# A two-layer macaron trunk on one core: joint hi|lo products in the feed-forward blocks, an unscaled up half, and both tiles' down products in one row

## The chip, the cores and the metric

The kernel runs on one core of one Trainium2 chip. The metric is device microseconds of one execution, the median of several runs. The engines are named as the profile names them: PE is TensorE (PEld its weight loads), DVE is VectorE, ACT is ScalarE, POOL is GpSimd, SP is the queue from which all weights are fetched.

## What is computed

The reference is two layers, each a half-step gated feed-forward block, a token mixer (a causal convolution module in layer 0, a gated linear recurrence in layer 1) and a second feed-forward block, all with a norm ahead and a norm behind. The sequence has 256 tokens of width 1024, and the inner width of a feed-forward block is 2816. What the change touches:

```python
def rms_norm(x, gain):
    y = x32 * lax.rsqrt(jnp.mean(x32 * x32, axis=-1, keepdims=True) + EPS)
    return (y * gain)
def swiglu_ffn(x, w_in, w_out):
    gate, up = jnp.split(x @ w_in, 2, axis=-1)
    return (jax.nn.silu(gate) * up) @ w_out
...
for layer in range(DEPTH):
    h = swiglu_ffn(rms_norm(x, g[0]), ffn_w_in[layer, 0], ffn_w_out[layer, 0])
    x = x + 0.5 * rms_norm(h, g[1])
    ...                                   # token mixer
    h = swiglu_ffn(rms_norm(x, g[4]), ffn_w_in[layer, 1], ffn_w_out[layer, 1])
    x = x + 0.5 * rms_norm(h, g[5])
```

## The kernel before

**Numbers as pairs.** Every float32 operand of a large product is split into a rounded part and the rest (`split`, lines 131 to 133: one ACT cast to `wh` or `hi`, one DVE subtraction to `wl` or `lo`), and a product is three matmuls: hi·hi, hi·lo, lo·hi.

**Tiles.** The 256 tokens are two tiles of 128. `xth` and `xtl` (lines 100 and 101) hold the turned, gained but not yet normed input of a block, all 8 blocks k of 128 channels of tile 0 and then of tile 1; `xkh` and `xkl` are views that give block k of both tiles, so two pieces of 128 elements. The norm factor r of a token is applied to the products, not to the input.

**A feed-forward block** (`ffn`, from line 348) walks through 11 chunks of 256 inner channels. The weights of a chunk are six transfers of 128x1024 (`fetch`: four `w1`, two `w2`), each landing in a `raw` buffer (4 of them) and split into a `wh` and a `wl` buffer (10 each). Chunk 0 is multiplied with the tokens as rows (`project`, `up`, `turn`). Chunks 1 to 10 are multiplied with the channels as rows: `up_both(c, b)` with b = 0, 1 takes a block of 128 gate channels and the 128 up channels that belong to it. It calls `channels` (line 319), which makes, in the two halves of one PSUM bank `mm`, 24 matmuls each for gate and up: 8 blocks k times three matmuls of 256 columns. One DVE step (line 332) then multiplies both halves by the tokens' factors `scales` into `ga`. ACT takes the sigmoid (line 386), DVE multiplies twice (387, 388), and `split` makes the hidden pair in `both[c]`, a `b4` buffer. `down(t, c)` multiplies the hidden pair of tile t with `w2[c]`, 12 matmuls of 512 columns into two `acc` banks.

**Order.** The loop of line 419 writes `up_both(c, 0)`, `down(0, c-1)`, `up_both(c, 1)`, `down(1, c-1)`. A scheduler orders each engine's queue from this; PE, ACT, DVE and SP each run their own queue strictly in its order and wait for each other by semaphores. Within ACT's and DVE's queues the splits of coming weights stand between the steps that evacuate `channels`. PSUM has four `acc`, two `mm` and two `tr` banks; `tr` serves transposes, the spectrum of the convolution's taps in the first block, and small sums.

**Ends.** `post_norm` forms the closing norm of a block: ACT's sums of squares, a POOL addition of D·EPS and a power (`rsqrt`), then x is updated. `mean_square` makes the factor r of the next block on the same two engines, and `start` puts the two together. The recurrent mixer also calls `channels` (`forget`, `query`, 8 calls); the four feed-forward blocks call it 80 times.

Of the kernel before, what the change touches and what calls it, by code (L numbers as in the profile page):

```python
# [16 lines left out]
P = 128  # L17
# [23 lines left out]
def trunk_kernel(  # L41
# [33 lines left out]
    def narrow(tag, dtype=F32):  # L75
        return new(sb, [P, 256], dtype, tag, {"e": 4, "hid": 4}[tag])
# [75 lines left out]
    def mean_square(src):  # L152
# [7 lines left out]
        return rsqrt(tot, 1.0 / D, EPS)  # L160

    def pre_norm(t, gi):
        src = xs[t]
        hi, lo = xth[:, t * D : (t + 1) * D], xtl[:, t * D : (t + 1) * D]
        for h in range(2):
# [4 lines left out]
            for j in range(4):  # L170
                k = h * 4 + j
                g = gcol[:, gi * KD + k : gi * KD + k + 1]
                act.activation(hi[:, k * P : (k + 1) * P],
                               pt[:, j * P : (j + 1) * P], AF.Copy, scale=g)
            for j in range(4):
                k = h * 4 + j
                g = gcol[:, gi * KD + k : gi * KD + k + 1]
                sl = slice(k * P, (k + 1) * P)
                dve.scalar_tensor_tensor(
                    lo[:, sl], pt[:, j * P : (j + 1) * P], g, hi[:, sl].bitcast(F32),  # L180
# [4 lines left out]
    def boot():  # L185
# [14 lines left out]
        def turned(i):  # L200
            src = part(pieces, i)
            nc.sync.dma_start(src, x_turned[i])
            for j in range(2):
# [3 lines left out]
                act.activation(xkh[:, k], xk, AF.Copy, scale=g)  # L207
                dve.scalar_tensor_tensor(xkl[:, k], xk, g, xkh[:, k].bitcast(F32),
                                         op0=ALU.mult, op1=ALU.subtract)

        def multiply(t, i):
            wh, wl = ws[i]
            hi, lo = xth[:, t * D : (t + 1) * D], xtl[:, t * D : (t + 1) * D]
            for k in (2 * i, 2 * i + 1):
                sl = slice((k % 2) * 512, (k % 2) * 512 + 512)
                kp = slice(k * P, (k + 1) * P)
                mm3(o[t], hi[:, kp], lo[:, kp], wh[:, sl], wl[:, sl], k == 0, k == KD - 1)

        for i in range(4):
            with behind(act, dve, pe, nc.sync):  # L220
                turned(i)
# [7 lines left out]
            if i == 3:  # L229
                with behind(dve, pe):  # L230
# [5 lines left out]
                    pool.tensor_tensor(r, ms, mhalf[:, :NT], op=ALU.pow)  # L236
            with behind(pe):
                multiply(1, i)
        xt = [(xth[:, t * D : (t + 1) * D], xtl[:, t * D : (t + 1) * D], r[:, t : t + 1])
              for t in range(NT)]  # L240
# [14 lines left out]
    def post_norm(t, accs, gain, share, bias=None):  # L255
# [16 lines left out]
        r = rsqrt(ss[:, 0:1], ss[:, 1:2], D * EPS, op=ALU.add)  # L272
# [6 lines left out]
    def project(t, xt, ws):  # L279
        o = mm()  # L280
        hi, lo, _ = xt
        for h in range(2):
            todo = []
            for k in range(h * 4, h * 4 + 4):
                wh, wl = ws[k // 2]
                sl = slice((k % 2) * 512, (k % 2) * 512 + 512)
                kp = slice(k * P, (k + 1) * P)
                pe.matmul(o, hi[:, kp], wh[:, sl], start=k == 0, stop=False)  # L288
                pe.matmul(o, hi[:, kp], wl[:, sl], start=False, stop=False)  # L289
                todo.append((lo[:, kp], wh[:, sl]))  # L290
# [4 lines left out]
    def blocks(hi, lo, n):  # L295
        return [(hi[:, k * P : (k + 1) * P], lo[:, k * P : (k + 1) * P]) for k in range(n)]
# [22 lines left out]
    def channels(ws, cols_, scales):  # L319
        o = mm()  # L320
        for part in range(2):
            og = o[:, part * SEQ : (part + 1) * SEQ]
            for k in range(KD):
# [3 lines left out]
                pe.matmul(og, wh[:, cs], xkh[:, k], start=k == 0, stop=False)  # L327
                pe.matmul(og, wh[:, cs], xkl[:, k], start=False, stop=False)  # L328
                pe.matmul(og, wl[:, cs], xkh[:, k], start=False, stop=k == KD - 1)  # L329
# [6 lines left out]
    def start(gi, before):  # L336
# [4 lines left out]
        with behind(act):  # L341
            r = [mean_square(xs[0])]
        second = pre_norm(1, gi)
        with behind(act):
            r.append(mean_square(xs[1]))
        return [(*first, r[0]), (*second, r[1])]

    def ffn(layer, which, before, extra=None):
        base = layer * 3 + (0 if which == 0 else 2)
        accs = [None, None]  # L350
        w1, w2, hid, raw, both = {}, {}, {}, {}, {}
# [567 lines left out]
```

## Time and profile before

| | |
|---|---|
| time, median of 3 runs | 1020.4 us (1019.01 to 1020.74) |
| the profiled execution's own time | 1019.7 us |
| its span, first to last instruction | 1017.9 us |
| PE busy | 1003.4 us, 99% of the span |
| DVE, ACT busy | 711.0 us (70%), 503.3 us (49%) |
| mean granted TensorE clock | 0.995 |

Matmuls overlap in the records: one of 256 columns is 281 ns long on the average, but the next starts after less than half of that. How long a stage takes is therefore read from the starts of its first and of the next stage's first matmul, not from the sum of lengths. An engine's idle time counts only where PE then waits for it.

### The profile page before, as it was taken

The numbers are of one execution on the slowest core, as the hardware profiler recorded it, in microseconds if no ns is written. First come the engines' busy times: TensorE is split into PE (matmuls) and PEld (weight loads), VectorE is DVE, ScalarE is ACT, GpSimd is POOL, SyncE is SP. The second block draws the span as 40 slices with busy tenths as digits, with TensorE's granted clock in tenths as the row PEclk, the third lists the DMA queues.
The fourth block names the chain that finished last, engine by engine and source line by source line (L and its number), as shares of the span: only waits on it lengthen the run. The fifth ranks groups of instructions, "written<-read, shape, count | busy, mean of one in ns | idle before, by whom it ended". The sixth has DMA issues, their size and how long they took to land.

```text
span 1017.9 us, 16846 instructions
## 1 busy us (share of the span) xinstructions
PE 1003.4 (99%) x6692; PEld 916.1 (90%) x6692; DVE 711.0 (70%) x1114; ACT 503.3 (49%) x840; POOL 47.0 (5%) x85
## 2 busy tenths in 40 slices
PE   9999999999899999999999999999999999999997
PEld 7999999888779999999899999989998889999996
DVE  6766756899787575658675757687788595656563
ACT  7554534764485444446554535474143473535341
POOL 1000000010010000000200000020000110000000
PEclk9999999999899999999999999999999999999999
DMA  7885564742536565657455555665233565565541
GB/s 251 270 272 180 173 209 155 266 172 90 186 103 212 184 202 171 201 172 236 157 174 199 190 183 181 211 201 173 85 124 105 165 195 178 166 207 170 203 145 42
DMA packets 50958, 182.19 MB, mean 179 GB/s; under 512 B 6048, under 2 KB 6176, under 8 KB 50880
## 3 DMA queue, kind: packets, MB, share of 16 engines
q1 hardware_dynamic: 50736, 181.09, 53.8%
q8 instruction: 52, 0.85, 0.3%
q14 instruction: 26, 0.21, 0.1%
q10 hardware_dynamic: 144, 0.03, 0.0%
HBM read 180.06 MB, written 1.05 MB: 178 GB/s over the span
## 4 chain that ended last, share of the span: by engine, by line
PE 94%; DVE 2%; ACT 1%; DMA 1%; POOL 1%; issue 0%; DVEq 0%; POOLq 0%; SPq 0%; ACTq 0%
PE mm L327 16%; PE mm L328 16%; PE mm L329 16%; PE acc L137 9%; PE acc L136 9%; PE acc L138 9%; PE mm L288 4%; PE mm L289 4%; PE mm L292 4%; PE tr L630 2%; DMA raw<-wts 1%; PE tr L169 1%; DVE wl L133 1%; PE tr L136 1%; PE tr L138 1%; PE tr L137 1%
## 5 line engine op out<-in xcount | busy, mean ns | idle before, releaser
L133 DVE TENSOR_TENSOR wl<-raw,wh 128x1024 fp32r<-128x1024 f32 (+1 forms) x386 | 400.9, 1061 | 197.5 <-ACT wh L132 193.6
L132 ACT CAST wh<-raw 128x1024 fp32r<-128x1024 f32 (+1 forms) x386 | 337.5, 922 | 278.7 <-PE mm L328 128.8
L327 PE MATMUL mm<-xth,wh 128*128 128x256 f32 x1408 | 396.2, 281 | 0.3 <-ACT wh L132 0.3
L329 PE MATMUL mm<-xth,wl 128*128 128x256 f32 x1408 | 396.1, 281 | 0.0
L328 PE MATMUL mm<-xtl,wh 128*128 128x256 f32 x1408 | 396.0, 281 | 0.0
L327 PEld LDWEIGHTS mm<-xth,wh 128*128 128x128 f32 x1408 | 265.7, 189 | 3.8 <-DVE e L387 0.7
L328 PEld LDWEIGHTS mm<-xtl,wh 128*128 128x128 f32 x1408 | 265.1, 188 | 2.5
L329 PEld LDWEIGHTS mm<-xth,wl 128*128 128x128 f32 x1408 | 266.1, 189 | 0.1
L136 PE MATMUL acc<-wh,b 128*128 128x512 f32 x352 | 138.0, 392 | 0.0
L137 PE MATMUL acc<-wl,b 128*128 128x512 f32 x352 | 137.4, 390 | 0.0
L138 PE MATMUL acc<-wh,b 128*128 128x512 f32 x352 | 137.4, 390 | 0.0
L138 PEld LDWEIGHTS acc<-wh,b 128*128 128x128 f32 x352 | 66.1, 188 | 14.4
L136 PEld LDWEIGHTS acc<-wh,b 128*128 128x128 f32 x352 | 66.1, 188 | 11.4
L137 PEld LDWEIGHTS acc<-wl,b 128*128 128x128 f32 x352 | 66.1, 188 | 11.4
L386 ACT ACTIVATE e<-ga 128x256 f32<-128x256 f32 x80 | 33.4, 418 | 78.4 <-DVE ga L332 78.4
L288 PE MATMUL mm<-wh,xth 128*128 128x512 f32 x176 | 70.8, 402 | 0.0
L289 PE MATMUL mm<-wl,xth 128*128 128x512 f32 x176 | 70.0, 398 | 0.0
L332 DVE TENSOR_TENSOR ga<-mm,scales 128x512 f32<-128x512 f32 x88 | 60.4, 686 | 11.5 <-PE mm L329 11.4
L132 ACT CAST b<-e 128x256 fp32r<-128x256 f32 x80 | 32.4, 405 | 51.4 <-DVE e L388 51.4
L147 POOL TENSOR_SCALAR tiny<-tiny 128x1 f32<-128x1 f32 (+1 forms) x28 | 8.5, 302 | 918.8 <-ACT b L269 736.3
L292 PE MATMUL mm<-wh,xtl 128*128 128x512 f32 x176 | 49.3, 396 | 0.0
L133 DVE TENSOR_TENSOR b<-e,b 128x256 fp32r<-128x256 f32 x80 | 33.8, 423 | 20.8 <-ACT b L132 20.8
(164 smaller groups left out, 864.5 us busy)
## 6 DMA issues: line engine op xcount, KB each, us to landing
raw<-wts SPq DMA_DIRECT2D x328, 512.0 KB, 5.2
b<-rows SPq DMA_DIRECT2D x10, 512.0 KB, 6.8
b<-x_turned SPq DMA_DIRECT2D x4, 256.0 KB, 5.8
x<-x_in SPq DMA_DIRECT2D x2, 512.0 KB, 7.4
out_dram<-x SPq DMA_DIRECT2D x4, 256.0 KB, 2.0
b<-dft SPq DMA_DIRECT2D x1, 371.0 KB, 6.0
ca<-masks SPq DMA_DIRECT2D x1, 192.0 KB, 3.5
b<-w_dw SPq DMA_DIRECT2D x1, 128.0 KB, 6.2
```

The source lines that it names most:

```text
L132: act.copy(dst_h, src)
L133: dve.tensor_tensor(dst_l, src, dst_h.bitcast(F32), op=ALU.subtract)
L136: pe.matmul(o, lh, rh, start=first, stop=False)
L137: pe.matmul(o, lh, rl, start=False, stop=False)
L138: pe.matmul(o, ll, rh, start=False, stop=last)
L288: pe.matmul(o, hi[:, kp], wh[:, sl], start=k == 0, stop=False)
L289: pe.matmul(o, hi[:, kp], wl[:, sl], start=False, stop=False)
L292: pe.matmul(o, a, w, start=False, stop=h == 1 and n == 3)
L327: pe.matmul(og, wh[:, cs], xkh[:, k], start=k == 0, stop=False)
L328: pe.matmul(og, wh[:, cs], xkl[:, k], start=False, stop=False)
L329: pe.matmul(og, wl[:, cs], xkh[:, k], start=False, stop=k == KD - 1)
L332: dve.tensor_tensor(pair(res), pair(o), scales.unsqueeze(1).broadcast_to([P, 2, SEQ]), op=ALU.mult)
```

## The change

1. `xth` and `xtl` become one tile `xt` in the order block k, part (hi or lo), tile, so that hi and lo of block k for both tiles are 512 adjacent elements; `turned(t)` gives the views of one tile. Two unused tiles of 88 and 40 floats stand ahead of and behind it.
2. `channels` multiplies a hi weight block with the whole of these 512 columns (hi·hi in the left half of a bank, hi·lo in the right), 8 matmuls, and then the lo weight block with the 256 hi columns, 8 matmuls into the left half. Gate and up now have a bank each, `mm` and `tr`. ACT copies the right half to an `e` buffer, DVE adds it to the left, and only the gate is multiplied by `scales`. `e` has 6 buffers for 4. The mixer keeps the old form under the name `channel_pair`.
3. The up half thus stays without the factor r (in `up` too), so the hidden values and the sums of `down` are short of one factor r per token. The closing norm divides by the root of the mean square plus EPS, so it gives the same when EPS is divided by r squared: `mean_square` and `boot` store D·EPS times (mean square + EPS) in `floors`, one more POOL step per tile and block, and `post_norm` adds that in place of the constant.
4. The loop writes `up_both(c, 0)`, `up_both(c, 1)`, `down(0, c-1)`, `down(1, c-1)`.

```diff
-        return new(sb, [P, 256], dtype, tag, {"e": 4, "hid": 4}[tag])
+        return new(sb, [P, 256], dtype, tag, {"e": 6, "hid": 4}[tag])
...
-    xth = const.tile([P, NT * D], F32R, name="xth")
-    xtl = const.tile([P, NT * D], F32R, name="xtl")
-    xkh = xth.rearrange("p (t k m) -> p k t m", t=NT, m=P)
-    xkl = xtl.rearrange("p (t k m) -> p k t m", t=NT, m=P)
+    const.tile([P, 88], F32, name="before_xt")
+    xt_all = const.tile([P, NT * 2 * D], F32R, name="xt")
+    const.tile([P, 40], F32, name="after_xt")
+    xhl = xt_all.rearrange("p (k s t m) -> p k s t m", t=NT, s=2, m=P)
...
+    def turned(t):
+        return [xhl[:, :, s, t, :] for s in range(2)]
...
-    def rsqrt(ss, scalar, eps, n=1, op=ALU.mult):
+    def rsqrt(ss, scalar, eps, n=1, op=ALU.mult, floor=None):
         t = tiny(n)
         pool.tensor_scalar(t, ss, scalar, eps, op0=op, op1=ALU.add)
+        if floor is not None:
+            pool.tensor_scalar(floor, t, D * EPS, None, op0=ALU.mult)
...
-        r = rsqrt(ss[:, 0:1], ss[:, 1:2], D * EPS, op=ALU.add)
+        r = rsqrt(ss[:, 0:1], ss[:, 1:2], floor, op=ALU.add)
...
     def channels(ws, cols_, scales):
+        res = wide("ga")
+        for part, bank in enumerate((mm, tr)):
+            o = bank()
+            pair = o.rearrange("p (s t m) -> p s t m", s=2, m=P)
+            block = lambda w, k: w[:, (k % 2) * 512 + cols_[part] : (k % 2) * 512 + cols_[part] + P]
+            for k in range(KD):
+                pe.matmul(pair, block(ws[k // 2][0], k), xhl[:, k], start=k == 0, stop=False)
+            for k in range(KD):
+                pe.matmul(pair[:, 0], block(ws[k // 2][1], k), xhl[:, k, 0],
+                          start=False, stop=k == KD - 1)
+            cross = narrow("e")
+            act.copy(cross, o[:, SEQ:])
+            dve.tensor_tensor(res[:, part * SEQ : (part + 1) * SEQ], o[:, :SEQ], cross, op=ALU.add)
+        dve.tensor_tensor(res[:, :SEQ], res[:, :SEQ], scales, op=ALU.mult)
+        return res
+
+    def channel_pair(ws, cols_, scales):
         o = mm()
...
-            dve.scalar_tensor_tensor(h, o[:, CH:], r, g, op0=ALU.mult, op1=ALU.mult)
+            dve.tensor_tensor(h, o[:, CH:], g, op=ALU.mult)
...
             up_both(c, 0)
             if c == 1:
                 turn(1, 0)
+            up_both(c, 1)
             if c < NC - 1:
                 down(0, c - 1)
-            up_both(c, 1)
             if c < NC - 2:
                 down(1, c - 1)
...
-        post_norm(0, accs[0], gain, 0.5)
+        post_norm(0, accs[0], gain, 0.5, floor=floors[0])
```

How the instructions stand on the engines, in a chunk in the middle of a block. On PE before, the end of one block's product (the last of the 8 blocks k of its up half), the head of tile 0's down row, whose six rows for the second block of the hidden pair follow in the same way, and the next product's start:

```order
L327 MATMUL mm_3931<-xth,wh_3914 128x256
L328 MATMUL mm_3931<-xtl,wh_3914 128x256
L329 MATMUL mm_3931<-xth,wl_3915 128x256
L136 MATMUL acc_3459<-wh_3745,b_659_3755 128x512
L137 MATMUL acc_3459<-wl_3746,b_659_3755 128x512
L138 MATMUL acc_3459<-wh_3745,b_659_3755 128x512
...
L327 MATMUL mm_4000<-xth,wh_3896 128x256
L328 MATMUL mm_4000<-xtl,wh_3896 128x256
L329 MATMUL mm_4000<-xth,wl_3897 128x256
```

On PE after, the up half of the second block's product, the heads of the rows of tile 0 (`acc_3327`) and tile 1 (`acc_3341`), and the next chunk's first product:

```order
L331 MATMUL tr_3932<-xt,wh_3828 128x512 x2
L331 MATMUL tr_3932<-xt,wh_3834 128x512 x2
L331 MATMUL tr_3932<-xt,wh_3840 128x512 x2
L331 MATMUL tr_3932<-xt,wh_3846 128x512 x2
L333 MATMUL tr_3932<-xt,wl_3829 128x256 x2
...
L140 MATMUL acc_3327<-wh_3695,b_766_3705 128x512
...
L140 MATMUL acc_3341<-wh_3695,b_766_3705 128x512
...
L331 MATMUL mm_4021<-xt,wh_3985 128x512 x2
L331 MATMUL mm_4021<-xt,wh_3991 128x512 x2
```

A product's 24 matmuls of one half have become 8 wide and 8 narrow ones, all hi weights are used before the first lo weight, and 24 matmuls of `down` stand together between two chunks.

On ACT, one chunk's work before (casts of weights `wh`, sigmoids `e`, casts of the hidden pair `b`):

```order
L132 CAST b_784_4630<-e_4682 128x256
L132 CAST wh_4783<-raw_4781 128x1024
L132 CAST wh_4789<-raw_4787 128x1024
L132 CAST wh_4795<-raw_4793 128x1024
L132 CAST wh_4801<-raw_4799 128x1024
L386 ACTIVATE e_4751<-ga_4749 128x256
L132 CAST wh_4934<-raw_4932 128x1024
L132 CAST b_784_4630<-e_4751 128x256
```

And after, from the copy of the second product's gate half on:

```order
L336 COPY e_3929<-mm_3912 128x256
L136 CAST wh_3997<-raw_3995 128x1024
L136 CAST wh_4003<-raw_4001 128x1024
L136 CAST wh_4009<-raw_4007 128x1024
L336 COPY e_3949<-tr_3932 128x256
L410 ACTIVATE e_3953<-ga_3911 128x256
L136 CAST wh_4015<-raw_4013 128x1024
L136 CAST b_797_3862<-e_3953 128x256
L136 CAST wh_4142<-raw_4140 128x1024
```

The copy of the up half (`tr_3932`) now stands behind three casts of the next chunk's weights, and the sigmoid behind that copy.

## Rows read from the trace of the kernel before

**Rows 1.** Page, busy time: us, share of the span, instructions of each engine.
```profile
PE 1003.4 (99%) x6692; PEld 916.1 (90%) x6692; DVE 711.0 (70%) x1114; ACT 503.3 (49%) x840; POOL 47.0 (5%) x85
```

**Rows 2.** Page, chain that ended last, its shares of the span by engine.
```profile
PE 94%; DVE 2%; ACT 1%; DMA 1%; POOL 1%; issue 0%; DVEq 0%; POOLq 0%; SPq 0%; ACTq 0%
```

**Rows 3.** Windows, second block's chunks: from:to, length, busy per engine, clock, DMA share, GB/s.
```profile
310.00:480.00 170.00, 170.00 (x1201) 159.84 (x1201) 110.44 (x153) 80.05 (x114) 0.88 (x2) 1.00 0.60 197
```

**Rows 4.** Timeline, PE, where products and down rows begin: start, us, engine, line, what.
```profile
333.70 0.28 PE L327 MATMUL mm<-xth,wh 128*128 128x256 f32 x1
...
339.40 0.40 PE L136 MATMUL acc<-wh,b 128*128 128x512 f32 x1
...
342.14 0.28 PE L327 MATMUL mm<-xth,wh 128*128 128x256 f32 x1
...
347.84 0.40 PE L136 MATMUL acc<-wh,b 128*128 128x512 f32 x1
...
350.58 0.28 PE L327 MATMUL mm<-xth,wh 128*128 128x256 f32 x1
...
354.74 0.28 PE L329 MATMUL mm<-xth,wl 128*128 128x256 f32 x1
354.85 0.28 PE L327 MATMUL mm<-xth,wh 128*128 128x256 f32 x1
```

**Rows 5.** Chain in order of time: start, us, projection and convolution matmuls.
```profile
217.77 0.24 PE tr L136 x2
...
830.02 0.93 PE mm L292 x4
```

**Rows 6.** Groups by form: line, engine, what, count, busy us, mean ns, idle before; last: timeline.
```profile
L133 DVE TENSOR_TENSOR wl<-raw,wh 128x1024 fp32r<-128x1024 f32 x270 | 326.0, 1222 | 188.9 <-ACT wh L132 187.5
L132 ACT CAST wh<-raw 128x1024 fp32r<-128x1024 f32 x270 | 272.0, 1050 | 251.7 <-PE mm L328 126.8 <-DMA raw<-wts 106.4 <-PE mm L292 8.3
L332 DVE TENSOR_TENSOR ga<-mm,scales 128x512 f32<-128x512 f32 x88 | 60.4, 686 | 11.5 <-PE mm L329 11.4
L387 DVE TENSOR_TENSOR e<-e,ga 128x256 f32<-128x256 f32 x80 | 33.8, 423 | 18.7 <-ACT e L386 18.7
L502 DVE TENSOR_TENSOR b<-tr,b 128x256 f32<-128x256 f32 x8 | 3.4, 422 | 2.1 <-PE tr L138 2.0
...
310.56 0.36 ACT L316 COPY scales<-tr 128x256 f32<-128x256 f32 x1
```

**Rows 7.** Timeline, ACT and DVE, weight splits of one chunk; in brackets the idle before.
```profile
337.39 3.90 ACT L132 CAST wh<-raw 128x1024 fp32r<-128x1024 f32 x4 [3.12 <-PE mm L328]
...
338.47 2.36 DVE L133 TENSOR_TENSOR wl<-raw,wh 128x1024 fp32r<-128x1024 f32 x2 [3.74 <-ACT wh L132]
```

**Rows 8.** Page, DMA issues: count, KB each, us from issue to landing.
```profile
raw<-wts SPq DMA_DIRECT2D x328, 512.0 KB, 5.2
```

**Rows 9.** Timeline, start of the second block's chunk 1 on PE, ACT and DVE.
```profile
307.64 0.37 PE L327 MATMUL mm<-xth,wh 128*128 128x256 f32 x1
...
312.79 1.06 ACT L132 CAST wh<-raw 128x1024 fp32r<-128x1024 f32 x1 [0.20 <-DMA raw<-wts]
...
312.62 2.48 DVE L133 TENSOR_TENSOR wl<-raw,wh 128x1024 fp32r<-128x1024 f32 x2 [0.72 <-ACT wh L132]
```

**Rows 10.** Timeline, first block's chunks 1 and 2 on PE, ACT and DVE.
```profile
19.11 0.28 PE L327 MATMUL mm<-xth,wh 128*128 128x256 f32 x1
...
19.56 1.13 ACT L132 CAST wh<-raw 128x512 fp32r<-128x512 f32 x2
...
20.96 2.17 ACT L132 CAST wh<-raw 128x512 fp32r<-128x512 f32 x4
...
37.02 1.05 ACT L132 CAST wh<-raw 128x1024 fp32r<-128x1024 f32 x1 [0.41 <-DMA raw<-wts]
...
37.84 0.28 PE L327 MATMUL mm<-xth,wh 128*128 128x256 f32 x1
```

More of the change, by code (lines that the diff above doesn't have):

```diff
@@ L172, in pre_norm @@
                 g = gcol[:, gi * KD + k : gi * KD + k + 1]
-                act.activation(hi[:, k * P : (k + 1) * P],
-                               pt[:, j * P : (j + 1) * P], AF.Copy, scale=g)
+                act.activation(hi[:, k], pt[:, j * P : (j + 1) * P], AF.Copy, scale=g)
             for j in range(4):
@@ L183, in pre_norm, with boot @@
         return hi, lo
-    def boot():
+    def boot(floors):
         pieces = [b4(), b4()]
@@ L236, in boot @@
                     pool.tensor_tensor(r, ms, mhalf[:, :NT], op=ALU.pow)
+                    for t in range(NT):
+                        pool.tensor_scalar(floors[t], ms[:, t : t + 1], D * EPS, None, op0=ALU.mult)
             with behind(pe):
                 multiply(1, i)
-        xt = [(xth[:, t * D : (t + 1) * D], xtl[:, t * D : (t + 1) * D], r[:, t : t + 1])
-              for t in range(NT)]
+        xt = [(*turned(t), r[:, t : t + 1]) for t in range(NT)]
         return xt, ws, o
@@ L253, in transposed, with post_norm @@
                                      op0=ALU.mult, op1=ALU.subtract)
-    def post_norm(t, accs, gain, share, bias=None):
+    def post_norm(t, accs, gain, share, bias=None, floor=D * EPS):
         ss = tiny(2)
@@ L286, in project @@
                 sl = slice((k % 2) * 512, (k % 2) * 512 + 512)
[L287 to L290, printed above, removed]
+                pe.matmul(o, hi[:, k], wh[:, sl], start=k == 0, stop=False)
+                pe.matmul(o, hi[:, k], wl[:, sl], start=False, stop=False)
+                todo.append((lo[:, k], wh[:, sl]))
             for n, (a, w) in enumerate(todo):
@@ L295, in blocks @@
     def blocks(hi, lo, n):
+        if len(hi.shape) == 3:
+            return [(hi[:, k], lo[:, k]) for k in range(n)]
         return [(hi[:, k * P : (k + 1) * P], lo[:, k * P : (k + 1) * P]) for k in range(n)]
@@ L326, in channels @@
                 cs = slice(col, col + P)
-                pe.matmul(og, wh[:, cs], xkh[:, k], start=k == 0, stop=False)
-                pe.matmul(og, wh[:, cs], xkl[:, k], start=False, stop=False)
-                pe.matmul(og, wl[:, cs], xkh[:, k], start=False, stop=k == KD - 1)
+                xh, xl = xhl[:, k, 0], xhl[:, k, 1]
+                pe.matmul(og, wh[:, cs], xh, start=k == 0, stop=False)
+                pe.matmul(og, wh[:, cs], xl, start=False, stop=False)
+                pe.matmul(og, wl[:, cs], xh, start=False, stop=k == KD - 1)
         res = wide("ga")
@@ L334, in channels, with start @@
         return res
-    def start(gi, before):
+    def start(gi, before, floors=(None, None)):
         before(0)
@@ L341, in start @@
         with behind(act):
-            r = [mean_square(xs[0])]
+            r = [mean_square(xs[0], floors[0])]
         second = pre_norm(1, gi)
         with behind(act):
-            r.append(mean_square(xs[1]))
+            r.append(mean_square(xs[1], floors[1]))
         return [(*first, r[0]), (*second, r[1])]
@@ L351, in ffn @@
         w1, w2, hid, raw, both = {}, {}, {}, {}, {}
+        floors = [new(sb, [P, 1], F32, "floor", 4) for _ in range(NT)]
         if before is None:
-            xt, w1[0], o = boot()
+            xt, w1[0], o = boot(floors)
         else:
-            xt = start(base, before)
+            xt = start(base, before, floors)
         def fetch(c):
@@ L442, in rest @@
                 expand(accs[1], xks, ws, False, True, slice(1, None))
-                post_norm(1, accs[1], gain, 0.5)
+                post_norm(1, accs[1], gain, 0.5, floor=floors[1])
         return rest
@@ L534, in turn @@
                     dve.tensor_tensor(y[:, bs], y[:, bs], s[:, bs], op=ALU.mult)
-                    sl = slice(h * 512 + a, h * 512 + a + step)
-                    split(hi[:, sl], lo[:, sl], y[:, bs])
+                    ks = slice((h * 512 + a) // P, (h * 512 + a + step) // P)
+                    split(hi[:, ks], lo[:, ks], y[:, bs].rearrange("p (k m) -> p k m", m=P))
             return hi, lo
@@ L576, in forget @@
             for pr in range(2):
-                xf = channels(ws, (2 * pr * P, (2 * pr + 1) * P), scales)
+                xf = channel_pair(ws, (2 * pr * P, (2 * pr + 1) * P), scales)
                 sl = slice(pr * 512, (pr + 1) * 512)
@@ L591, in query @@
             for pr in range(2):
-                xq = channels(ws, (2 * pr * P, (2 * pr + 1) * P), scales)
+                xq = channel_pair(ws, (2 * pr * P, (2 * pr + 1) * P), scales)
                 sl = slice(pr * 512, (pr + 1) * 512)
```

24 lines of the change are left out of this document (11 added, 13 removed).

## The prediction, made blind

> **What bounds the kernel now.** I read the page's busy shares first: PE is busy for 1003.4 of 1017.9 us [rows 1]. Busy time alone proves little for overlapping matmuls, so the chain of work that ended last comes next: 94% of it is PE, 2% DVE, 1% DMA [rows 2]. The stage that matters is the middle of a feed-forward block, and there the windows show 170.00 us of PE in 170.00 us at clock 1.00, while DVE works 110.44 us and ACT 80.05 us [rows 3]. So in the four blocks PE never waits; only fewer or shorter PE spacings can shorten them, and other engines' work costs nothing until PE must wait for it.
>
> The spacing comes from the timeline [rows 4]. A product `channels` begins at 333.70 and the down row behind it at 339.40: 5.70 us for 48 matmuls of 256 columns, **118.75 ns** each (two neighbours, 354.74 and 354.85, stand 110 ns apart). The down row lasts until 342.14: 2.74 us for 12 matmuls of 512 columns, **228.3 ns** each. The same place recurs at 350.58, so a chunk takes 16.88 us.
>
> **Part 1, the joint products.** Columns stay as they are (16 x 512 + 16 x 256 = 48 x 256); 16 pairs of narrow matmuls become 16 wide ones. A pair costs 237.5 ns, a wide one 228.3 ns by the down row: 9.2 ns less. There are 80 calls (4 blocks, 10 chunks, 2 products), so 1280 x 9.2 ns = **11.8 us less**, all of it on PE and so on the path. A product becomes 16 x 228.3 + 16 x 118.75 ns = 5.55 us, a chunk 2 x 5.55 + 5.48 = 16.58 us.
>
> No row shows a 512-wide matmul that streams the x tile, so the price has bounds. The nearest other row is the projection, 512 wide with x as the stationary operand: 0.93 us for four, 232.5 ns [rows 5]; by it the gain is 1280 x 5.0 = 6.4 us. I take the down row, since there as here a split weight tile and an activation tile from SBUF meet, and keep both ends. The narrow matmuls now read 256 adjacent elements instead of two pieces; the convolution's products do that today at 0.24 us for two [rows 5], so I count no gain, though 115 ns instead of 118.75 would give another 4.8 us (the 110 ns neighbours say that it is possible).
>
> The Trainium skill ("TensorE: Matmul & The Clock Gate", Back-to-back issue gap) gives a fixed cost of about 2.5 ns per matmul at full clock on top of its columns. By it the 1280 matmuls that go would save an estimated 3.2 us instead of 11.8. The trace disagrees: from 118.75 and 228.3 ns [rows 4] a line through both has 9.2 ns at zero columns.
>
> **The x tile's place.** The diff moves x in its partition. If the 4.2 ns between projection and down row come from where x stands, the 528 projection matmuls (22 calls of 24) gain up to 2.2 us; nothing shows that they do. I take half, **1.1 us less**, with 0 and 2.2 as bounds.
>
> **Part 2, evacuation.** DVE's one step of 686 ns becomes three of 256 columns (two additions out of PSUM as line 502's, 422 ns; one product as line 387's, 423 ns), and ACT gets two copies like line 316's of 0.36 us [rows 6]. Per chunk DVE goes from 6 x 1.222 + 2 x (0.686 + 3 x 0.42) = 11.2 us to 6 x 1.222 + 12 x 0.42 = 12.4 us, ACT from 8.0 to 9.4 us, in a PE chunk of 16.58 us. Both still fit, but their queues run in order, so the deadlines count. I follow one chunk by hand from t = 0, where PE starts the up half of the second product.
>
> PE ends that half at 2.77, the down rows at 8.25 and starts the next chunk's product there. ACT: gate copy until 0.5; then casts of the next chunk's third and fourth w1 and first w2, whose buffers are freed by this very half, from 0.65 at 0.96 us each (3.90 us for four, [rows 7]) until 3.55; up copy 3.9, sigmoid 4.3, fourth cast 5.3. DVE: addition and scaling of the gate until 1.3; the split of the third w1 must wait for the lo weights of the half, about 2.2, and ends at 3.35, the fourth at 4.5 (2.36 us for two); then the up half's addition at 4.9. PE wants the third weight's hi part at 8.25 + 4 x 0.228 = 9.2 (ready 1.6) and its lo part at 8.25 + 1.83 + 0.48 = 10.6 (ready 3.35), the fourth's at 10.8 (ready 4.5): **6 us of slack**, more than now, because both down rows stand in between. In the old order the four casts began 3.12 us after ACT had run dry and the next product started 4.75 us after them (337.39 to 342.14). The up half's bank `tr` is wanted again at 8.25 + 5.55 = 13.8 (free at 4.9). The next two w1 reuse raw buffers freed at 3.35 and 4.5; with 5.2 us per transfer [rows 8] they land at 8.6 and 9.7, are split by 10.7 and 11.8, and are wanted a chunk later. The first product of the next chunk ends at 13.8 and its hidden pair is ready at 16.3, before the cycle closes at 16.58. So no wait on PE: **0 us**. What hides the 1.2 us of DVE work is DVE's own waits; without that cover it would be 40 x 1.2 = 48 us.
>
> **Part 3, order.** Two down rows together cost the same 24 matmuls. They give each second product's evacuation 5.5 us of cover instead of 2.7. Nothing else is queued differently on SP. **0 us.**
>
> **Part 4, floors.** One more POOL step per tile and block, 0.44 us each by the window of [rows 3], between the sum of squares and the power. The factor r is first wanted after a projection of 24 x 232.5 ns = 5.6 us, so PE does not feel it; the unscaled `up` is a step of the same size. **0 us.**
>
> **Starts of blocks.** In blocks 2 to 4 both products of chunk 1 need the same `tr` bank, since `turn` takes the other. The first product's up half starts at about 307.64 + 2.77 + 0.44 = 310.85 and ends at 313.6; its copy waits for the cast of 312.79 until 314.2, its addition for the splits of 312.62 until 315.5 [rows 9]; the bank is wanted at about 316.7: 1.2 us of slack. In block 1 all weights come just in time. The hi-first order needs the second pair of blocks 0.46 us after 19.11 instead of 0.71 us, while its two casts run from 19.56 to 20.7 and the next four from 20.96 [rows 10]: about 0.5 us lost. Chunk 2's fourth w1 is cast at 37.02, waiting for its DMA, and PE began there at 37.84 [rows 10]; with three more DVE steps ahead of its split I give another 0.5 us. Together **1.0 us more**, bounds 0 and 2.
>
> **Sum.** Against the profiled execution's own 1019.7 us: -11.8 - 1.1 + 1.0 = 1007.8. It lies 0.7 us under the median of the three runs, so the forecast is **1008.5 us**. Its own bounds: 1019.7 - 11.8 - 2.2 - 4.8 = 1000.9 if everything falls out well, and with the projection's rate and 2 us of start, 1020.4 - 6.4 + 2 = 1016.
>
> **Rivals.**
> Pairs save next to nothing: the wide matmul stands at 235 ns, halfway between the projection's 232.5 and two narrow ones' 237.5. Then 1280 x 2.5 = 3.2 us go and 1.0 us comes: 1020.4 - 2.2, about 1018. For it: the columns are the same. Against it: 228.3 ns in the down row, whose operands are of the same types and widths. Chance 6%. (The Trainium skill's rule of Part 1 would have the same outcome.)
>
> Wide matmuls at the projection's 232.5 ns: 1020.4 - 6.4 + 1 = 1015. For it: x is the one operand that both share. Chance 10%.
>
> Slower: PE waits for a bank. It is the `tr` bank of the second product's up half; DVE's addition that frees it stands behind two weight splits and ACT's copy behind three casts. It decides when that addition comes later than 13.8 in the count above, 9 us later than I find, for instance since a transfer or an in-order wait that I have overlooked holds ACT's casts. A wait of 0.45 us in each of the 36 chunks from the second on is 16 us, against 12.9 gained and 1.0 lost: 1020.4 + 4.3, about 1025. Against it: DVE idles 35% of the window [rows 3]. Chance 7%.
>
> **How the numbers follow.** Forecast with its bounds (1002 to 1014): 76%; the projection's rate 10%; fixed cost 6%; bank wait 7%; the last 1% is that nothing moves. The range 1002 to 1015 leaves out the fixed cost, the bank wait and some of the tails. Faster by over 0.2% (below 1018.4; about what a measurement of this kernel can tell from no change) holds the first two and half of the third: 0.89. Same: half of the third, the last, a little of the bank wait: 0.05. Slower: 0.06.
>
> **What would show it.** Right: in the middle of a block a chunk of 16.5 to 16.7 us, wide matmuls 227 to 230 ns apart, PE still 170 in 170, the waits of ACT and DVE larger in number but no idle time of PE in front of `tr` or of the fourth w1. The first block would gain about 2 us, the other three about 3 us each. Wrong: wide spacings of 232 ns or more; a PE wait for DVE's addition out of `tr`, or for a weight split at a chunk's start; a loss of over 2 us before 60 us.

## The result and the profile after

The changed kernel takes **1014.5 us** (median of 4 runs, 1013.5 to 1014.9); the kernel before takes 1019.7 us on the same chip. The ratio is 0.9947, with a 95% interval from 0.9935 to 0.9960: **5.2 us faster**, where 11.9 were forecast. The time is just inside the forecast's range of 1002 to 1015 us; the saving is less than half of the forecast one. The profiled executions agree: their spans are 1017.9 and 1012.6 us.

The page of the changed kernel, its busy times and the chain's shares by engine (compare [rows 1, 2]), and the window of the second block (columns as in [rows 3]):

```profile
PE 997.6 (99%) x5412; PEld 853.8 (84%) x5412; DVE 750.1 (74%) x1274; ACT 548.2 (54%) x1000; POOL 56.3 (6%) x93
...
PE 91%; ACT 2%; DVE 2%; DMA 2%; POOL 1%; issue 1%; POOLq 0%; DVEq 0%; SPq 0%; ACTq 0%
```

```profile
310.00:480.00 170.00, 170.00 (x899) 145.68 (x898) 122.19 (x194) 92.69 (x157) 0.95 (x2) 1.00 0.59 198
```

DVE has 11.75 us and ACT 12.64 us more work in this window than before, and PE still works 170.00 of 170.00 us. So the evacuation is covered, as forecast. What PE does with its time is in the chain (start, us, engine, bank and line, how many matmuls); one chunk, with the halves of its first product (the second one reads the same), the first of its 24 down matmuls and the next chunk's start:

```profile
341.99 1.86 PE mm L331 x8
343.85 0.95 PE mm L333 x8
344.80 1.86 PE tr L331 x8
346.65 0.94 PE tr L333 x8
...
353.22 0.23 PE acc L140
...
358.67 1.86 PE mm L331 x8
```

Eight wide matmuls take 1.86 us, **232.5 ns each**, not the 228.3 of the down row; 232 or more is what the forecast itself gave as a sign of being wrong. A chunk lasts from 341.99 to 358.67: 16.68 us, where 16.88 was read before [rows 4] and 16.58 forecast.

The whole span can be counted in the same way. From the starts of all matmuls in the trace, each matmul has the time until the next start; up to 1.25 times the median of its width counts as its spacing, what is above as waiting:

| kernel | 256-column matmuls | 512-column matmuls | waiting |
|---|---|---|---|
| before | 519.8 us (4368) | 422.4 us (1823) | 16.3 us |
| changed | 215.8 us (1808) | 720.2 us (3103) | 17.2 us |

By the differences of the two columns, the 2560 narrow matmuls that went took 304.0 us, **237.5 ns a pair**, just as forecast, and the 1280 wide ones that came took 297.8 us, **232.7 ns each**. That is 6.2 us gained and 0.9 us of waiting added: 5.3 us, the difference of the spans.

### The profile page after: what moved, and what is told of

The parts are those of the page before. It is cut to its first block, busy times and chain, and to the rows that moved or that the text cites. A ratio compares the mean times of both kernels' runs of the same rounds, so it can differ in the third digit from the quotient of the medians.

```text
span 1012.6 us, 14787 instructions
## 1 busy us (share of the span) xinstructions
PE 997.6 (99%) x5412; PEld 853.8 (84%) x5412; DVE 750.1 (74%) x1274; ACT 548.2 (54%) x1000; POOL 56.3 (6%) x93
## 4 chain that ended last, share of the span: by engine, by line
PE 91%; ACT 2%; DVE 2%; DMA 2%; POOL 1%; issue 1%; POOLq 0%; DVEq 0%; SPq 0%; ACTq 0%
PE mm L331 15%; PE tr L331 15%; PE acc L141 9%; PE acc L142 9%; PE acc L140 9%; PE mm L333 8%; PE tr L333 7%; PE mm L295 3%; PE mm L291 3%; PE mm L292 3%; PE tr L654 2%; DMA raw<-wts 2%; PE mm L351 2%; PE mm L352 2%; PE mm L350 1%; DVE wl L137 1%
## 5 line engine op out<-in xcount | busy, mean ns | idle before, releaser
L331 PE MATMUL mm<-xt,wh 128*128 128x512 f32 x640 | 164.1, 397 | 0.5 <-ACT wh L136 0.5
L331 PE MATMUL tr<-xt,wh 128*128 128x512 f32 x640 | 162.1, 395 | 0.0
L331 PEld LDWEIGHTS mm<-xt,wh 128*128 128x128 f32 x640 | 116.7, 188 | 25.7 <-ACT wh L136 1.3
L331 PEld LDWEIGHTS tr<-xt,wh 128*128 128x128 f32 x640 | 114.9, 188 | 20.9
L333 PEld LDWEIGHTS mm<-xt,wl 128*128 128x128 f32 x640 | 87.4, 188 | 7.4 <-DVE wl L137 0.2
L333 PEld LDWEIGHTS tr<-xt,wl 128*128 128x128 f32 x640 | 87.0, 188 | 7.4
L333 PE MATMUL mm<-xt,wl 128*128 128x256 f32 x640 | 90.0, 282 | 0.0
L333 PE MATMUL tr<-xt,wl 128*128 128x256 f32 x640 | 88.6, 281 | 0.0
L291 PE MATMUL mm<-wh,xt 128*128 128x512 f32 x176 | 70.7, 402 | 0.0
L292 PE MATMUL mm<-wl,xt 128*128 128x512 f32 x176 | 69.8, 397 | 0.0
```

The lines of the kernel that those rows point to most:

```text
L291: pe.matmul(o, hi[:, k], wh[:, sl], start=k == 0, stop=False)
L292: pe.matmul(o, hi[:, k], wl[:, sl], start=False, stop=False)
L331: pe.matmul(pair, block(ws[k // 2][0], k), xhl[:, k], start=k == 0, stop=False)
L333: pe.matmul(pair[:, 0], block(ws[k // 2][1], k), xhl[:, k, 0], start=False, stop=k == KD - 1)
```

## The experiments

There were four theories for the 232.7 ns. P: where the operands stand in their partition. S: a new stationary operand for each matmul. C: traffic of the other engines. X: x as an operand. P became theory R in the second group of experiments, when it could be said which places: what counts is the difference between the places of a matmul's two operands.

**The prices by themselves.** Behind the last store, rows like these, with the operands varied:

```diff
+ if case == 0: pe.matmul(quad, st(wh, k), xhl[:, k], ...)
+ elif case == 1: pe.matmul(quad, st(wh, 0), xhl[:, k], ...)
+ elif case == 2: pe.matmul(quad, st(wh, k), xhl[:, 0], ...)
...
+ else: pe.matmul(o, blk(k), half(wh[4 + n % 2], k), ...)
```

> The changed kernel with nine rows of 64 products each behind its last store (cases 0 to 8; about 140 us more in all), which measure the price of one matmul while the other engines have nothing to do; what they compute is thrown away. Case 0 is the joint product as the kernel has it (weights' blocks as stationary operand, x hi|lo moving, 512 columns), case 1 the same with one stationary block throughout, case 2 with one moving block throughout, case 3 with the blocks in the order 0 2 4 6 1 3 5 7, case 4 the pair as two matmuls of 256 columns, case 5 the projection (x stationary, weights moving), case 6 blocks of a hidden tile stationary and x moving, case 7 a hidden block used twice in a row with weights moving (two thirds of a down row), case 8 a new hidden block each time with weights moving. Theory P (where the operands stand in their partition makes the 233 to 235 ns): cases 0 and 3 differ by 2 ns or more, and cases 1 or 2 fall to 228. Theory S (a new stationary operand each time costs): case 0 at 233, case 1 and case 7 at 228, case 8 at 232 or more. Theory C (the other engines' traffic costs): every 512-wide case at 226 to 228 here, although case 0 stands at 233 to 235 in the blocks. Theory X (x as an operand costs): cases 0, 1, 2, 3, 5, 6 at 232 or more, 7 and 8 at 228. Case 4 gives 237 to 240 ns a pair by all of them.

The chain of that kernel, lines 853 to 870 being cases 0 to 8:

```profile
1007.14 14.93 PE mm L853 x64
1022.07 14.93 PE tr L855 x64
1037.00 14.93 PE mm L857 x64
1051.93 14.93 PE tr L859 x64
1066.87 15.20 PE mm L862 x128
1082.07 14.88 PE tr L864 x64
1096.95 14.87 PE mm L866 x64
1111.82 14.56 PE tr L868 x64
1126.38 14.51 PE mm L870 x64
```

Divided by the 64 products, cases 0 to 3 take 233.3 ns, the projection's form (case 5) 232.5, x behind a hidden block (case 6) 232.3, and weights behind a hidden block 226.7 (case 8), although there the stationary operand changes each time. So C falls for wide matmuls (no other engine has work here to speak of) and S falls (case 1 keeps its stationary block and is as slow as case 0). P in the form written there falls too: it is not this or that block, since case 2 with one moving block is as slow. What is left is x, or something that all blocks of x share, such as the start of its tile.

**x where it stood.** The two pads go:

```diff
-    const.tile([P, 88], F32, name="before_xt")
...
-    const.tile([P, 40], F32, name="after_xt")
```

> The changed kernel without the two pads beside the x tile, so that x begins where it began in the kernel before (and all behind it moves down by 512 bytes). Theory P: joint products' spacing moves by 1 ns or more, that is the time by 1.3 us or more, in either direction (if the pads were well chosen, 1016 to 1020 us). Theories S, C and X: the spacing stays at 233 to 235 ns and the time within 0.5 us of the changed kernel's 1014.5.

1015.2 us (1013.7 to 1016.7): no difference that can be told. In the trace the 512-column matmuls stand 0.9 ns further apart than in the changed kernel and the 256-column ones 1.4 ns closer, so the place does act, in opposite directions.

**Pairs apart.**

```diff
-                pe.matmul(pair, block(ws[k // 2][0], k), xhl[:, k], start=k == 0, stop=False)
+                for s in range(2):
+                    pe.matmul(pair[:, s], block(ws[k // 2][0], k), xhl[:, k, s],
+                              start=k == 0 and s == 0, stop=False)
```

> The changed kernel with each joint matmul of 512 columns written as two of 256 (hi, then lo, same stationary block); order, evacuation, banks and floors stay. It isolates the merge of the pairs. By the forecast's price (228.3 against 237.5 ns) the merge is worth 11.8 us: 1026. By the spacing read after the change (about 234 against 237.5) it is worth 4.5 us: 1019, and then the rest of the change is worth about nothing. If the pair in the new order costs less than 237.5 ns, the merge is worth less still, and the rest of the change brought something.

1026.4 us (1025.6 to 1027.4). The forecast's 1026 is met, but not by its working. Counted as above, the pair costs 241.1 ns here and not 237.5, the wide one 232.7: in this kernel the merge is worth 10.8 us of spacing, and 6.8 us separate this kernel from the one before. Of these, 4.6 are spacing of the 4368 narrow matmuls (524.4 against 519.8 us). The chain shows them at 1.92 us for 16, 120 ns each, against 118.75 before [rows 4]. The eight of the lo weights behind them stand at 120 ns as well, so the difference of 241.1 ns holds a little of these; the pair by itself is 240 ns:

```profile
344.83 1.92 PE mm L332 x16
346.75 0.96 PE mm L335 x8
```

**The old order of the rows.**

```diff
-            up_both(c, 1)
             if c < NC - 1:
                 down(0, c - 1)
+            up_both(c, 1)
```

> The changed kernel with the first tile's down row between the two products again, as in the kernel before. It isolates the order of the rows. Theory that the order costs and gives nothing while evacuation stays covered (the forecast): 1014 to 1015 us, PE full in the middle of a block. Rival, that the order carries the evacuation: idle time of PE in front of the second product's bank or weights, 0.2 to 0.5 us a chunk, 1022 to 1034 us. Second rival, that the new order itself costs at the blocks' starts: 1 to 2 us faster, 1012 to 1013.

1014.9 us (1014.3 to 1015.7): the order costs and gives nothing, and the evacuation doesn't need it.

**Offsets.** The built program puts x at byte 26144 of its partition, the hi weights at 104608 + 4096 n and the hidden tiles at 47264 + 4096 n. Modulo 2048 bytes weights and hidden tiles agree; x doesn't.

```diff
+ if kind == "a": pe.matmul(o, w[:, at : at + P], t[:, d : d + 512], ...)
+ elif kind == "b": pe.matmul(o[:, :SEQ], w[:, at : at + P], t[:, d : d + SEQ], ...)
+ elif kind == "c": pe.matmul(o, t[:, at + d : at + d + P], w[:, at : at + 512], ...)
+ else: pe.matmul(o, w[:, at + d : at + d + P], t[:, d : d + 512], ...)
```

> The changed kernel with 29 rows of 32 products each behind its last store (about 190 us more), while the other engines have nothing to do; what they compute is thrown away. The operands are blocks of weight tiles and activation tiles whose places in the partition agree modulo 2048 bytes. Kind a is the joint product's form (weights stationary, 512 columns moving from the activation tile, that start d elements behind its start), kind b the same with 256 columns, kind c the projection's form (128 columns stationary at d, weights moving), for d = 0, 8, 16, 32, 64, 96, 128, 256, 352; kind d shifts both operands by 8 or 96 elements. In the changed kernel the x tile and the weights are 352 elements apart modulo 512. Theory R (what counts is how the two operands' places differ): a and c at 226 to 228 ns for d = 0, 128 and 256, 232 or more at 96 and 352, and kind d at 226 to 228 for both shifts. Theory M (the moving operand's own place counts): kind d as slow as kind a at the same d, and kind c the same at every d. Theory X (it is because it is x, whatever its place): all cases at 226 to 228 ns.

The chain; lines 850, 852, 854 and 856 are kinds a, b, c and d. The rows are d = 8 and 16, then 64, 96 and 256, then kind d at 8 and 96:

```profile
1031.74 7.47 PE tr L850 x32
1039.21 3.78 PE mm L852 x32
1042.99 7.47 PE tr L854 x32
1050.45 7.32 PE mm L850 x32
1057.78 3.77 PE tr L852 x32
1061.55 7.47 PE mm L854 x32
...
1087.67 7.28 PE mm L850 x32
1094.95 3.83 PE tr L852 x32
1098.79 7.28 PE mm L854 x32
1106.07 7.46 PE tr L850 x32
1113.52 3.80 PE mm L852 x32
1117.33 7.44 PE tr L854 x32
...
1143.16 7.25 PE tr L850 x32
1150.41 3.83 PE mm L852 x32
...
1180.22 7.30 PE tr L856 x32
1187.52 7.30 PE mm L856 x32
```

At d = 64 and 256 (and 128) the wide matmul takes 7.25 to 7.28 us for 32, **226.6 to 227.5 ns**; at 8 and 96 it takes 7.46 to 7.47, **233 ns**; shifted together (kind d), 7.30, that is 228.1 ns with about ten dearer matmuls at the row's head and 226.6 behind them. At d = 16 the joint product's form has 7.32 (228.8 ns) and the projection's 7.47. The first row of all, kind a at d = 0, is not counted: PE waits in it, and the granted clock there was 0.87. So it is the difference of the two places that counts, modulo 64 elements or 256 bytes, for the joint product's form and for the projection's. X and M fall, theory R holds. For 256 columns it goes the other way: 3.83 us (119.7 ns) in agreement, 3.78 to 3.80 (118 to 119) otherwise. By the built programs, x and weights are 32 elements apart modulo 64 in the changed kernel and 40 in the kernel before; the hidden tiles of the down row, from which the price of the forecast was taken, are 0 apart.

**x in agreement.**

```diff
-    const.tile([P, 88], F32, name="before_xt")
+    const.tile([P, 120], F32, name="before_xt")
...
-    const.tile([P, 40], F32, name="after_xt")
+    const.tile([P, 8], F32, name="after_xt")
```

> The changed kernel with the x tile 128 bytes further on (32 elements of the second pad go into the first), so that its place agrees with that of the weights and hidden tiles modulo 512 bytes; nothing else moves. Theory R (the difference of the places counts): joint products fall from about 234 to 227 ns (1280 x 7 = 9 us), projections from 232 to 227 (528 x 5 = 2.6 us), the 256-wide ones by some ns (some 1900 of them at up to 4 ns, 0 to 8 us): 994 to 1004 us. Theory X (it is x as such): joint products stay at 233 to 235 ns, 1013.5 to 1015.5 us. Rival A (the pads stood in a good place): slower, 1016 to 1020 us.

**1009.5 us** (1008.7 to 1010.0), ratio 0.9893 to the kernel before, with an interval from 0.9873 to 0.9912: faster than both kernels, by 5.0 us than the changed one. It is called the aligned kernel from here on. The theory's 994 to 1004 is missed, and the chain shows why:

```profile
356.47 1.81 PE mm L331 x8
358.29 0.95 PE mm L333 x8
359.24 1.84 PE tr L331 x8
...
373.09 1.81 PE mm L331 x8
```

Behind a down row, eight wide matmuls take 1.81 us (226.6 ns each). Behind narrow ones, as in three of a chunk's four rows of eight, they take 1.84: the starts stand 233, 236, 228, 232, 231 ns apart and only then 227. And the narrow ones gain nothing, as their own rows of the offsets study would have said. All 512-column spacing falls from 720.2 to 713.7 us, the 256-column one rises from 215.8 to 216.8.

**The kernel before, in agreement.**

```diff
+    const.tile([P, 24], F32, name="before_xt")
     xth = const.tile([P, NT * D], F32R, name="xth")
     xtl = const.tile([P, NT * D], F32R, name="xtl")
+    const.tile([P, 40], F32, name="after_xt")
```

> The kernel before with pads of 24 and 40 elements beside its two x tiles, so that their places agree with those of the weights modulo 256 bytes (they were 40 elements apart modulo 64); the weights move by 256 bytes with them, nothing else changes. Theory R by the rows of the offsets study (512 columns: 232 to 233 ns apart in place, 227 in agreement; 256 columns: 118 to 119 apart, 119.8 in agreement): the projections gain 528 x 5 = 2.6 us, the 4224 narrow matmuls lose 0.7 ns each, 3 us: 1018.5 to 1021.5 us, no difference that counts. So the agreement pays only together with the joint products. Rival (agreement helps every matmul, and the change has nothing to do with it): 1013 to 1016 us.

1022.95 us (1022.2 to 1024.4): **slower** by 3.3 us. The sign against the rival is clear; the size is past the range. The narrow matmuls take 525.2 us for 519.8 (1.2 ns each, not 0.7), the 512-column ones gain 2.2 us (420.2 for 422.4), about what was expected of the projections, and 1.5 us of waiting come on top; but the execution that was profiled took 1024.4 us, 1.5 above the median, so this waiting may be its own. So the agreement pays only together with the wide matmuls. Between the two kernels in agreement the change brings 1022.95 - 1009.53 = 13.4 us.

**Wides together.**

```diff
+        for part in range(2):
+            for k in range(KD):
+                pe.matmul(pairs[part], block(ws[k // 2][0], k, part), xhl[:, k], ...)
+        for part in range(2):
+            for k in range(KD):
+                pe.matmul(pairs[part][:, 0], block(ws[k // 2][1], k, part), xhl[:, k, 0], ...)
...
```

> The changed kernel with the x tile in agreement, and in each product first the 16 matmuls of 512 columns of both halves, then the 16 of 256, so that two passages from narrow to wide of four in a chunk go. Theory T (after a run of narrow matmuls the first five wide ones together take 27 to 28 ns more; the aligned kernel's rows show 233 236 228 232 231 and then 227): 40 chunks x 2 x 28 ns = 2.2 us less than the aligned kernel's 1009.5: 1007.3. Rival 1 (the passage is not what costs): 1009.5. Rival 2 (the gate half now leaves its bank 1.8 us later and the evacuation of both halves comes together, so that PE waits for a bank): 1011 to 1016.

1009.5 us (1009.0 to 1010.2), no gain in the sum. Theory T has its 2.1 us in the 512-column spacing (711.6 for 713.7), but waiting rises from 17.6 to 19.7 us and the narrow ones by 0.7. One of the new waits, at the start of the second block, in the chain:

```profile
305.70 5.38 DMA raw<-wts
...
311.15 1.06 ACT wh L136
...
312.24 1.23 DVE wl L137
313.47 0.68 DVE ga L339 x2
...
314.18 2.11 PE tr L331 x8
```

The two additions that free the banks now come together, behind a weight split that waits for its transfer, and PE waits for them until 314.18, about 0.6 us. That is the mechanism of the forecast's bank wait, here at one place instead of in each chunk. Most of the other new waits stand at the transposes of x behind the ends of blocks 1 to 3, where PE waits for DVE, and in the convolution; why they grow was not followed up.

**The mixer joint too**, in the recurrent mixer (HGRN in the expectation), with `channel_pair` calling the same function, on top of the wides together:

```diff
     def channel_pair(ws, cols_, scales):
+        return channels(ws, cols_, scales, True)
...
```

> As the kernel with the wide matmuls of both halves together, and the eight products of the HGRN mixer joint as well, by the same function. By the aligned prices a call goes from 48 x 120 = 5.76 us to 16 x 226.7 + 0.03 + 16 x 119.5 = 5.57 us: 8 x 0.19 = 1.5 us less, about 1005.8, if the longer evacuation (two copies and two additions more) lies beside other work. Rival (the mixer's chain runs through these evacuations): 0.3 to 1 us more a call at the calls that end a chain, 1007 to 1012.

1025.1 us (1023.8 to 1026.9), 15.6 us slower than without it, more than the rival said. Windows of the mixer's first scores, in the kernel with the wides together and then in this one (this one also with two sets of sixteen score matmuls by themselves), and the chain of this one:

```profile
705.00:745.00 40.00, 40.00 (x326) 38.24 (x325) 32.94 (x49) 11.62 (x15) 0.00 (x0) 1.00 0.30 106
```

```profile
705.00:745.00 40.00, 32.23 (x186) 29.24 (x186) 21.31 (x35) 2.70 (x6) 0.00 (x0) 0.74 0.11 40
...
724.90:726.90 2.00, 1.98 (x17) 1.86 (x16) 0.49 (x1) 0.00 (x0) 0.00 (x0) 1.00 0.00 0
728.40:732.00 3.60, 3.60 (x16) 3.43 (x16) 0.44 (x1) 0.00 (x0) 0.00 (x0) 0.50 0.00 0
```

```profile
724.92 1.98 PE tr L645 x16
...
726.93 0.69 DVE b L647
727.62 0.61 DVE b L649
...
728.37 3.66 PE tr L645 x16
```

The score matmuls (line 645) write to `tr` banks, and between two levels of them PE waits 1.5 us for DVE. The products filled these gaps, since they needed only an `mm` bank; the joint one needs a `tr` bank too. Then PE stands idle, and after several such gaps the sixteen matmuls at 728.37 run at a granted clock of 0.50, the lower level of 1.2 GHz, and take 3.66 us instead of 1.98. One gap alone didn't do it: the level that began at 712.28, also behind 1.48 us of idling, still ran at 1.00.

**Pairs apart, in agreement.** The edit of the pairs apart with the pads of 120 and 8.

> The changed kernel with the x tile in agreement (as in the aligned kernel, 1009.5 us) and each joint matmul written as two of 256 columns. It prices the merge where the operands agree. Theory R: two narrow matmuls at 120 ns each against one wide at 231 (mean, with the passages from narrow to wide in it): 1280 x 9 = 11.5 us slower than the aligned kernel, 1020.5 to 1022, near the kernel before in agreement (1022.95), so that the rest of the change is worth about nothing there. Rival (the merge is worth 11.9 us out of agreement as in agreement for another reason, and x's place brings its 5 us to any matmul): 1026.4 - 5 = 1021.4 as well; what tells the two apart is the spacing, flat at 120 ns by theory R, 117 to 123 in turn by the rival.

1024.4 us (1024.3 to 1025.8), 14.9 us above the aligned kernel, more than the 11 to 12.5 expected; the spacings inside a product are flat at 120 ns, which is theory R's sign. Counted over the span, a pair costs 241.2 ns and a wide matmul 230.2: 11.0 ns and 14.0 us. I had taken the wide mean from the products' records with their waits in it.

**x 256 bytes back.** Pads of 56 and 72 elements instead of 120 and 8.

> The aligned kernel with the x tile 256 bytes nearer to the start (64 elements of the first pad go into the second), so that the places agree modulo 256 bytes and no longer modulo 512. Theory R with 256 bytes, as the offsets study's row at d = 64 has it: 1009 to 1010 us, the first matmuls of 512 columns behind a down row at 226 to 227 ns. Rival (512 bytes or one lucky place): back at 233 ns and 1013.5 to 1015.5 us.

1010.3 us (1009.4 to 1010.5), and behind a down row eight wide matmuls take 1.81 us again, 226.6 ns each: the period is 256 bytes and not 512, and the first place was not a lucky one.

```profile
356.60 1.81 PE mm L331 x8
```

**The mixer joint in two `mm` banks.**

```diff
-        for part, bank in enumerate((mm, tr)):
+        for part, bank in enumerate(banks):
...
+        return channels(ws, cols_, scales, (mm, mm), True)
```

> The aligned kernel (1009.5 us) with the eight products of the HGRN mixer joint, this time with both halves in mm banks, so that no tr bank is asked for, which the scores hold. Theory F (in the kernel with the mixer joint the products could no longer fill PE between the score levels, for want of a tr bank; that was its 15.6 us): PE is busy again through the scores, and a call goes from 48 x 120 = 5.76 us to 2 x 2.79 = 5.59 us, 8 x 0.17 = 1.4 us less, about 1008. Rival (two mm banks of two leave no second buffer, and the evacuation by a copy and an addition stands in the scores' DVE queue): PE idles again between the levels, 1011 to 1022 us.

1013.8 us (1013.3 to 1015.2). Theory F is right about the main cause, as 11.3 of the 15.6 us come back; part of them is the clock, which stays at 1.00 in this window. (This edit starts from the aligned kernel, the one before from the wides together; both take 1009.5 us.) But the rival decides: the window has idle time still, and the edit loses 4.3 us against the aligned kernel.

```profile
705.00:745.00 40.00, 36.75 (x267) 32.96 (x266) 31.50 (x53) 13.28 (x21) 0.00 (x0) 1.00 0.22 79
```

## Why the prediction was right in its direction and wrong in its size

**The term that was mis-sized is the price of a wide matmul.** It was 228.3 ns by the down row; 232.7 is what the trace has. Of the 11.8 us of that term 6.2 came; the pair's 237.5 ns were right. The step that failed is "I take the down row, since there as here a split weight tile and an activation tile from SBUF meet". That was a likeness of kinds. The likeness that counts was in the addresses: the down row's operands agree modulo 256 bytes, x and the weights don't, neither before nor after. The number of the second rival, the projection's 232.5 ns and 1015 us, to which 10% were given, is the one that came true. Its reason was half right: x is what both share, but it is where x stands and not x as such, for with x in agreement the same matmul takes 226.6 ns behind a down row. So the place makes 2.5 of the 4.4 ns of the miss (232.7 to 230.2). Much of the rest is in what stands ahead: even in agreement the mean is 230.2 ns and not 228.3, as three of a chunk's four rows of wide matmuls begin behind narrow ones and have the dearer start, while the down row had it once in its twelve.

**In agreement the change is worth what was forecast, but by other prices.** Between the two kernels in agreement it brings 13.4 us, near the forecast 11.9, and that is partly chance. Out of agreement a pair is cheap (237.5 ns) and a wide matmul dear (232.7); in agreement it is the reverse (241.2 and 230.2). The forecast put the cheap pair of the one state against the cheap wide matmul of the other.

The traces have no fixed saving per pair at all: 4.8 ns from the kernel before to the changed one, 8.4 ns in the changed kernel's own order, 11.0 ns in agreement. So the line through two points, 9.2 ns at zero columns, was not a fixed cost either. The Trainium skill ("TensorE: Matmul & The Clock Gate", Back-to-back issue gap) has about 2.5 ns per matmul at full clock, an estimated 3.2 us for the 1280 that went. The traces don't agree with it: all three values are larger, and they change with the operands' places.

**The adjacent 256 elements**, 0 us with up to 4.8 us as a bound: right at 0. The lo weights' rows of eight take 0.94 to 0.95 us, 118 to 119 ns each, as before. The convolution's 0.24 us for two, by which no gain was counted, was the right row to take.

**The x tile's place**, 1.1 us by the forecast, gave 0: the projections stand 232 ns apart (median) in both traces, since the move went from one difference out of agreement to another. The idea was sound (in the kernel before put in agreement they stand 227 ns apart), the move just wasn't that one.

**Evacuation, 0 us**: right. PE is full in the window above, and ACT's and DVE's longer queues cost nothing in the middle of a block. **Order, 0 us**: right, by the run with the rows apart. **Floors, 0 us**: the added step takes 0.43 us where 0.44 were counted, and nothing in the traces speaks against the 0; it was not tried alone.

**Starts, 1.0 us**: half of it came. Of the 0.9 us of waiting more in the table, 0.5 lies ahead of block 1's end and next to none at the starts of the other blocks; that the sum is near 1.0 is chance. The first wait stands where it was forecast, in block 1 (timeline, PE; in brackets the idle before):

```profile
19.52 0.62 PE L331 MATMUL mm<-xt,wh 128*128 128x512 f32 x2
20.66 1.26 PE L331 MATMUL mm<-xt,wh 128*128 128x512 f32 x3 [0.51 <-ACT wh L136]
```

By the starts of its second chunk, PE is 0.35 us later than before (38.19 for the 37.84 of [rows 10]). Block 1 gains 0.7 us to its end, where about 2 were forecast, and the other three 1.8, 1.5 and 1.9, where about 3 each were. The convolution loses 0.7 us between its two ends, which the forecast didn't have. Counted as in the table, 0.6 of that is waiting (9.0 us against 8.4), but what makes the waits longer is not shown.

**The slower rival**, the bank wait, didn't come; the run with the wides together shows its mechanism at one place, the start of block 2, where PE does not wait in the changed kernel.

What stays open: why a pair in hi-then-lo order costs 240 ns or more in the changed kernel and 237.5 before. Neither the place (32 for 40 elements) nor the form (256 adjacent elements for two pieces of 128) makes it alone, for case 4 of the prices has the changed kernel's place and form and takes 15.20 us for 64 pairs, 237.5 ns each. What differs there is that the other engines are idle and no lo weights come between. Also open is by what mechanism the difference of two places acts on the spacing.

## What to carry to other kernels

A matmul's price is copied from a row only with its operands' addresses: look at where stationary and moving tile start, modulo 256 bytes, before taking one line's spacing for another's. After an edit that changes the width of a matmul, try the place again: here 32 elements of padding were worth as much as the change itself, and the same agreement cost 3.3 us in the kernel before. And an operation that seems to have slack may be the filler of another stage's gaps; which bank it needs then decides.

## What the runs showed of the hardware

- In the offsets study, 512-column matmuls stand 226.6 to 228.1 ns apart, as the mean of a row, when both operands' places agree modulo 256 bytes, and 232 to 233.4 ns when they are 8, 32 or 96 elements off. At 16 elements it was 228.8 with the activation tile moving and 233.4 with it stationary. For 256 columns the agreement is the slower state there, 119.7 against 117.8 to 118.8 ns; in the kernel with the pairs apart they stood at 120 ns out of agreement too.
- Out of agreement the spacing has a rhythm that doesn't come from the blocks: 238 and 229 ns in turn in the prices' cases 0 to 3, so with one stationary or one moving block throughout as well. In the changed kernel the gate half has this rhythm and the up half another one, from 228 to 241 ns, with the same difference of places. In agreement it is flat.
- With the operands in agreement, the first five wide matmuls behind a run of narrow ones take 27 ns more in all, in products and in down rows alike. Behind wide ones with another difference of places there is such a start too: 7.28 us at d = 64, behind a row out of agreement, for 7.25 at d = 256, behind one in agreement.
- An edit that opens gaps on PE can be paid twice: after several gaps of 1.5 us between score levels the granted clock stood at 0.50 for sixteen matmuls, 3.66 us for 1.98, and at 0.74 over 40 us with 32.23 us of PE work.
